# A hybrid encoder layer on one core: a staged opening, a third PSUM bank for projections, and a job order that passes blocked jobs

## The chip, the cores and the metric

The kernel runs on one core of one Trainium2 chip. The time is the device time of one execution in microseconds; here it is told as the median of several runs. The core has five engines, each with its own instruction queue, worked in order: TensorE (matmul, PE in the rows), VectorE (DVE), ScalarE (ACT), GpSimd (POOL) and SyncE (SP), which issues the DMA transfers. Matmuls write to PSUM, which has eight banks; VectorE and ScalarE read them from there.

## The reference

One step of a one-layer streaming encoder for 1024 prompt rows and 64 rows of a running stream, model width 1024, all in float32:

```
mod = silu(c) @ w_ada + b_ada           -> sh1, sc1, gt1, sh2, sc2, gt2
h   = rmsnorm(x) * (1 + sc1) + sh1
P   = h @ w_in                           # q, k, v | x, B, C | z gates | decays | merge gates
q, k, v, xs, B, C = silu(causal_dwconv4(...))
o   = gated_delta(l2norm(q), l2norm(k), v, g, beta)     # 8 heads, chunked, triangular solve
o   = rms(o) * gdn_norm * silu(z_g)
y   = ssd(xs, dt, A, B, C) + D * xs                     # 32 heads in 8 groups, chunked
y   = rms(y * silu(z_s)) * ssd_norm
x   = x + gt1 * (sigmoid(ga) * (o @ P_a) + sigmoid(gb) * (y @ P_b)) @ w_out
h2  = rmsnorm(x) * (1 + sc2) + sh2
u_a, u_v = causal_dwconv3(h2 @ w_up)
x   = x + gt2 * (silu(u_a) * u_v) @ w_down
return rmsnorm_final(x), and the new states of convolutions, delta net and SSD
```

## The kernel before

Both streams stand side by side as 1088 columns, channels on partitions. A projection makes 128 output channels: for each of three column segments (364, 364, 360) eight k tiles, and for each of these three matmuls, since weights and activations are split into two fp32r parts (high and low) and the product of the two low parts is left out. So a projection is 72 matmuls, a segment 24, and each segment fills one PSUM bank, which its `evac` reads.

**Opening.** x (eight tiles of 128 channels) is loaded first, then the weights of the modulation, in groups of four 512 KB loads. Each x tile is squared on ScalarE, and TensorE sums all eight squares over partitions with a matrix of ones, in fp32. From the sums come r0 = rsqrt (Ln and Exp). `ada` makes a modulation group: 32 matmuls per load pair, a copy, a transpose, an add. `norm_mod` makes the two parts of h for one x tile. The first two projections (`early_w`: the decays' small weights and the first K) run k tile by k tile while h comes, two k tiles (a pair) after each modulation group.

**Phase 1.** A list of jobs, one projection each: K, Q, V of the eight delta-net heads, B, C, X, x of the eight SSD groups, and 40 gate projections (24 z gates, 16 merge gates), which depend on nothing. The convolution of a mixer job runs in its `evac` on ScalarE and VectorE. Between the matmuls of the jobs stand the mixers' own matmuls: for each head an inverse (`gdn_inverse`: three kk batches, a 32-wide triangular solve on VectorE, four block steps), a scan over nine chunks (`gdn_scan`), the norm of o (`o_norm`, with a sum over partitions in `rsqrt_row`), for each group `ssd_mix`. Only TensorE's order is written out by hand: `weave` runs these generators against a planned clock, in which a step is due when the time in the table `LAT` has passed since its last one. `pick` chooses the next job: the first of the list when its condition holds, else a gate, up to `AHEAD` (3) gates more than the list's own F places; then the blocked job all the same. The other engines' orders come from a list scheduler.

PSUM before: two banks pj for projections, one each gk, gs (delta net), sa, sy (SSD), n and nv (kk batches, block steps and modulation, in turn).

**After phase 1** the gated outputs are multiplied by the two branch matrices and `w_out` (`project`, with `bank()` giving the banks in turn), then follow the norm, `up`, the convolution and `down`. The sums of the norms there used n and nv.

Of the kernel before, what the change touches and what calls it, by code (L numbers as in the profile page):

```python
# [20 lines left out]
P = 128  # L21
# [3 lines left out]
NC = 9  # L25
# [8 lines left out]
LAT = {"pre": 9.5, "dec": 1.6, "dec2": 27.6, "g0": 0.8, "e": 11.0, "kk": 1.0, "solve": 68.0, "inv": 1.8,  # L34
       "r": 1.6, "u": 1.7, "s": 2.5, "on": 18.4, "v": 9.0, "e2": 27.6, "s0": 5.6, "d0": 5.0, "w": 6.0, "r1": 2.0, "r2": 2.0}
MAN = {mybir.EngineType.PE}
ORDER = ["KFBFQCFXFxFV", "FKBFQCXFxFV"]
LAST = "BCFXx" + "F" * 9
AHEAD = 3
# [8 lines left out]
def body(tc, I, O):  # L48
# [34 lines left out]
    act.activation(scil, ct, AF.Tanh, scale=0.5)  # L83
# [9 lines left out]
    def ada(sc, g, ws, row, tag):  # L93
# [3 lines left out]
        for k0 in range(0, KT, 2):  # L97
            w = ws()
            sp.dma_start(w, I["wada"][g, :, k0:k0 + 2, :])
# [167 lines left out]
    def project_steps(w, x, evac):  # L267
# [5 lines left out]
        for si, (s, e) in enumerate(SEGS):  # L273
            ps = tl(pp, [P, 364], "pj", bufs=2)
# [43 lines left out]
    with ExitStack() as c1:  # L318
# [6 lines left out]
        hx = [tl(hp, [P, 2, T], f"h{k}", F32R) for k in range(KT)]  # L325
# [9 lines left out]
        for k in range(KT):  # L335
            sp.dma_start(xs[k], I["xT"][k])
# [3 lines left out]
        wb = [tl(gp, [P, TW], "k", bufs=2) for _ in range(2)] + [tl(gp, [P, 1024], "Ub"), tl(gp, [P, TW], "q", bufs=2)]  # L340
        wb += [sgt("bm"), tl(gp, [P, TC], "NU", bufs=2)]
        wb = [w[:, 0:1024].rearrange("p (k c) -> p k c", c=512) for w in wb]
        nwb = [0]

        def next_wb():
            nwb[0] += 1
            return wb[(nwb[0] - 1) % len(wb)]
        sc = padded_silu(tl(sg, [P, 256], "xw", bufs=2))
        r0 = tl(gp, [P, TC], "NU", bufs=2)
        a1 = tl(cst, [P, KT, 2], "a1")  # L350
        early_w = []
        with tc.manual_schedule(engines=MAN):
            nps = [tl(pp, [P, 364], t) for t in ("gs", "sa", "sy")]
            for k in range(KT):
# [6 lines left out]
            early = [[tl(pp, [P, 364], t, bufs=2 if t == "pj" else 1) for t in tags]  # L361
                     for tags in (("pj", "pj", "gk"), ("gs", "sa", "sy"))]
            for p in range(5):
                if p < 4:
                    ada(sc, p, next_wb, tl(gp, [P, P], "r"), "nv")
                    norm_scale(a1, wnm, 0, p)
                if p == 0:
                    early_w += [load_w(I["wsmall"]), load_w(I["win"][K0])]
                    continue
                ks = (2 * p - 2, 2 * p - 1)  # L370
                for k in ks:
                    for s, e in SEGS:
                        norm_mod(hx[k], xs[k], xs[k], r0, a1, k, 0, s, e, 0)
                for i in range(2):
                    for k in ks:
                        for si, (s, e) in enumerate(SEGS):
                            whi, wlo = early_w[i]
# [136 lines left out]
        def rsqrt_row(buf, eps):  # L514
# [3 lines left out]
            ps = tl(pp, [P, 364], "n")  # L518
# [20 lines left out]
        def kq_steps(w, h, j):  # L539
            yield from need(lambda: h < 2 or (heads[h - 2].norm.done if j else heads[h - 2].scanned))  # L540
# [763 lines left out]
```

## Time and profile before

| what | value |
|---|---|
| three runs, median (lowest to highest) | 2832.57 us (2831.6 to 2836.66) |
| profiled execution, its own time / span | 2831.39 / 2829.6 us |
| TensorE matmul busy | 2752.4 us, 97% of the span |
| VectorE / ScalarE / GpSimd busy | 1862.4 / 1247.5 / 201.9 us |
| moved by DMA | 266.75 MB |

Busy time is an average over stages with different limits. Phase 1 ends at about 1590 us; what follows is not touched but for the banks in which sums and modulation groups stand. In a stage where TensorE is busy nearly throughout, its gaps and the granted clock (1.00 is 2.4 GHz, half of it 1.2) are what is left to look at. A "releaser" is what ended a wait, inferred from the semaphores.

### The profile page before, as it was taken

How to read it: one execution, taken by the hardware profiler on the slowest of the kernel's cores; microseconds unless marked ns; L12 is line 12 of the kernel's file. 1: busy time of each engine (PE TensorE's matmuls, PEld its weight loads, DVE VectorE, ACT ScalarE, POOL GpSimd, SP SyncE). 2: the span in 40 equal slices, each digit the busy share in tenths (PEclk: the TensorE clock that was granted, in tenths of full speed). 3: DMA queues.
4: the chain of work that ended last, by engine and by line, in shares of the span. 5: the costliest groups of instructions: out<-in, count | busy, mean ns of one | idle time of the engine just before them, and what ended most of it. 6: DMA issues, size and time to landing. Idle time of an engine off the chain costs nothing.

```text
span 2829.6 us, 49056 instructions
## 1 busy us (share of the span) xinstructions
PE 2752.4 (97%) x18718; PEld 2654.6 (94%) x18718; DVE 1862.4 (66%) x4008; ACT 1247.5 (44%) x2847; POOL 201.9 (7%) x565
## 2 busy tenths in 40 slices
PE   7999999999999999999999999999999999999998
PEld 6999898999989999999999899999899999999998
DVE  4787687786877868678645657543675555555556
ACT  5634554554545444454443434312444242424244
POOL 0100111011101101111000000000010000000000
PEclk9999999999999999999999999999999999999999
DMA  6322313223232233222234766443211111111112
GB/s 221 96 74 76 117 53 117 70 82 104 81 97 81 82 94 99 78 85 79 79 99 146 245 204 204 139 147 93 90 47 49 45 46 38 53 38 53 38 60 72
DMA packets 204365, 266.75 MB, mean 94 GB/s; under 512 B 42522, under 2 KB 136410, under 8 KB 204130
## 3 DMA queue, kind: packets, MB, share of 16 engines
q1 hardware_dynamic: 204130, 263.62, 29.5%
q8 instruction: 147, 2.41, 0.4%
q14 instruction: 88, 0.72, 0.1%
HBM read 217.38 MB, written 46.13 MB: 93 GB/s over the span
## 4 chain that ended last, share of the span: by engine, by line
PE 80%; DVE 12%; DMA 4%; ACT 3%; issue 2%; POOL 0%; SPq 0%; DVEq 0%; ACTq 0%; POOLq 0%
PE pj L223 28%; PE pj L144 13%; PE gk L144 6%; PE gs L144 6%; PE sy L144 6%; PE sa L144 6%; PE sy L223 3%; DVE prod L615 3%; DVE Xb L618 2%; DMA wada<-in_wada 1%; PE gk L223 1%; DVE x L494 1%; PE n L223 1%; PE gs L223 1%; PE sa L227 1%
## 5 line engine op out<-in xcount | busy, mean ns | idle before, releaser
L223 PE MATMUL pj<-h,whi 128*128 128x364 f32 x4560 | 1157.5, 335 | 19.3 <-DVE fz L869 14.3
L223 PEld LDWEIGHTS pj<-h,whi 128*128 128x128 f32 x4560 | 792.9, 189 | 34.5 <-DVE fz L869 17.4
L223 PE MATMUL pj<-h,wlo 128*128 128x364 f32 x2280 | 749.2, 329 | 0.0
L223 PEld LDWEIGHTS pj<-h,wlo 128*128 128x128 f32 x2280 | 430.1, 189 | 0.0
L111 ACT CAST whi<-wraw 128x512 fp32r<-128x512 f32 (+1 forms) x386 | 234.5, 617 | 378.3 <-PE gs L144 145.5
L144 PE MATMUL pj<-op,whi 128*128 128x364 f32 (+1 forms) x1504 | 374.5, 329 | 0.0
L112 DVE TENSOR_TENSOR wlo<-wraw,whi 128x512 fp32r<-128x512 f32 (+1 forms) x386 | 263.0, 690 | 107.9 <-ACT whi L111 100.7
L144 PEld LDWEIGHTS pj<-op,whi 128*128 128x128 f32 x1504 | 266.5, 188 | 1.4 <-issue 0.2
L144 PE MATMUL pj<-op,wlo 128*128 128x364 f32 (+1 forms) x752 | 247.6, 329 | 0.0
L1096 DVE SCALAR_TENSOR_TENSOR acc<-buf,wfc,acc 128x364 f32<-128x364 f32 (+1 forms) x264 | 156.5, 596 | 97.9 <-ACT acc L1094 93.8
L144 PE MATMUL gk<-op,whi 128*128 128x364 f32 x752 | 191.2, 333 | 0.9 <-ACT op L185 0.6
L144 PE MATMUL gs<-op,whi 128*128 128x360 f32 x752 | 189.9, 331 | 0.0
L144 PE MATMUL sy<-op,whi 128*128 128x364 f32 x752 | 188.9, 331 | 0.0
L144 PE MATMUL sa<-op,whi 128*128 128x364 f32 x752 | 188.3, 330 | 0.0
L796 ACT ACTIVATE E<-E,ngam 128x128 f32<-128x128 f32 x288 | 96.4, 394 | 103.3 <-POOL E L793 101.9
L144 PEld LDWEIGHTS pj<-op,wlo 128*128 128x128 f32 x752 | 141.2, 188 | 0.5 <-issue 0.2
L144 PEld LDWEIGHTS gk<-op,whi 128*128 128x128 f32 x752 | 133.8, 189 | 4.6 <-DVE op L186 1.3
L144 PEld LDWEIGHTS gs<-op,whi 128*128 128x128 f32 x752 | 133.3, 188 | 2.6 <-ACT op L111 0.6
L144 PEld LDWEIGHTS sa<-op,whi 128*128 128x128 f32 x752 | 132.9, 188 | 2.2 <-issue 2.2
L144 PEld LDWEIGHTS sy<-op,whi 128*128 128x128 f32 x752 | 132.9, 188 | 2.1 <-issue 1.2
L615 DVE TENSOR_TENSOR prod<-Xb,Ub 108x2 f32<-108x2 f32 (+30 forms) x248 | 124.3, 501 | 5.6 <-POOL Ub L608 1.7
L144 PE MATMUL sa<-op,wlo 128*128 128x364 f32 x376 | 124.0, 330 | 0.0
(413 smaller groups left out, 4521.1 us busy)
## 6 DMA issues: line engine op xcount, KB each, us to landing
wraw<-in_win SPq DMA_DIRECT2D x160, 256.0 KB
wraw<-in_wup SPq DMA_DIRECT2D x88, 256.0 KB
gi<-gdr SPq DMA_DIRECT2D x72, 256.0 KB
wada<-in_wada SPq DMA_DIRECT2D x32, 512.0 KB
op<-spz SPq DMA_DIRECT2D x24, 544.0 KB
wraw<-in_wdown SPq DMA_DIRECT2D x40, 256.0 KB
spz<-fz SPq DMA_DIRECT2D x48, 182.0 KB
gt<-spg SPq DMA_DIRECT2D x48, 182.0 KB
```

The source lines that it names most:

```text
L111: act.copy(hi, src)
L112: dve.tensor_tensor(out=lo, in0=src, in1=hi, op=ALU.subtract)
L144: pe.matmul(pss[si][:, :e - s], lhsT=a[:, k, :], rhs=xk[:, b, s:e], start=(k == 0 and n == 0), stop=(k == nk - 1 and n == 2))
L223: pe.matmul(out, lhsT=lhsT, rhs=rhs, start=start, stop=stop)
L227: pe.transpose(out, in_, idn)
L494: dve.scalar_tensor_tensor(out=u, in0=buf[:, s + i:e + i], scalar=wcv[:, ti, i:i + 1], in1=u, op0=ALU.mult, op1=ALU.add)
L615: dve.tensor_tensor(out=prv, in0=X[:, 0:i + 1, 0:n].rearrange("p j c -> p c j"), in1=U[:, 0:i + 1, i:i + 1].rearrange("p j o -> p o j").to ...
L618: dve.tensor_reduce(out=X[:, i, 0:n], in_=prv, axis=mybir.AxisListType.X, op=ALU.add)
L796: act.activation(E[:, a, :], E[:, a, :], AF.Exp, bias=ngam[:, c, 8 + 4 * g + a:9 + 4 * g + a], scale=-1.0)
L1096: dve.scalar_tensor_tensor(out=acc[:, c0:c1], in0=buf[:, i + c0:i + c1], scalar=wfc[:, ti, i:i + 1], in1=acc[:, c0:c1], op0=ALU.mult, op1= ...
```

## The change

Opening: the first modulation group's weights are loaded ahead of x, into the places that later hold h; behind x come the two early weights whole, and then the other three groups' weights. The squares of x tiles 0 to 5 and of 6 and 7 are added on VectorE, and TensorE sums the two results: 6 matmuls for 24. The table of Ln and Exp is loaded once, right after the first Tanh. `norm_mod` works on all columns at once (1024 and 64) rather than by segment. The group of pair p+1 comes ahead of the matmuls of pair p.

Banks: nv goes, pj has three banks. The kk batches, block steps and modulation groups all use n; the sum under o's norm uses a pj bank; the sums of the output projections come from the rotation of `bank()`. The last two block steps leave out the ninth chunk, whose block is zero.

Order: `pick` passes a blocked job of one mixer and takes the first job of the other mixer that may go (never past a job of its own kind), then a gate, with up to six ahead. Some times of `LAT` are longer. In the order that comes of it, eleven gate projections follow the last mixer projection, where five did.

```diff
-LAT = {..., "kk": 1.0, "solve": 68.0, "inv": 1.8,
+LAT = {..., "kk": 1.6, "solve": 74.0, "inv": 2.6,
-AHEAD = 3
+AHEAD = 6
...
-        tag = ("pj", "gk", "pj", "gs", "sa", "sy")[nbank[0] % 6]
-        return tl(pp, [P, n], tag, bufs=2 if tag == "pj" else 1)
+        tag = ("pj", "gk", "pj", "gs", "pj", "sa", "sy")[nbank[0] % 7]
+        return tl(pp, [P, n], tag, bufs=3 if tag == "pj" else 1)
...
-            ps = tl(pp, [P, 364], "pj", bufs=2)
+            ps = tl(pp, [P, 364], "pj", bufs=3)
...
+        aw = [ada_w(0)]
+        for k in range(KT):
+            sp.dma_start(xs[k], I["xT"][k])
+        early_w = []
+        for src in (I["wsmall"], I["win"][K0]):
+            raw = tl(gp, [P, TW], "k", bufs=2)[:, 0:1024].rearrange("p (k c) -> p k c", c=P)
+            sp.dma_start(raw, src)
...
+        aw += [ada_w(p) for p in range(1, 4)]
+        inst = act.preload_act_table_set("natural_log_exp_and_others")
...
+            ada_h(0)
             for k in range(KT):
-                q = tl(cv, [P, 1096], "buf", bufs=2)
-                act.activation(q[:, 0:T], xs[k], AF.Square)
-                for si, (s, e) in enumerate(SEGS):
-                    pe.matmul(nps[si][:, :e - s], lhsT=ones, rhs=q[:, s:e], start=(k == 0), stop=(k == KT - 1))
+                k0 = 0 if k < 6 else 6
+                q = sq[k][:, 0:T] if k in sq else sqb[k % 4][:, 0:T]
+                act.activation(q, xs[k], AF.Square)
+                if k != k0:
+                    dve.tensor_tensor(out=sq[k0][:, 0:T], in0=sq[k0][:, 0:T], in1=q, op=ALU.add)
+                if k in (5, 7):
+                    for si, (s, e) in enumerate(SEGS):
+                        pe.matmul(nps[si][:, :e - s], lhsT=ones, rhs=sq[k0][:, s:e], start=(k == 5), stop=(k == 7))
...
+            for p in range(4):
+                for k in (2 * p, 2 * p + 1):
+                    hx.append(tl(hp, [P, 2, T], f"h{k}", F32R))
+                    norm_mod(hx[k], xs[k], xs[k], r0, a1, k, 0, 0, T, 0)
+                if p < 3:
+                    ada_h(p + 1)
...
-            ps = tl(pp, [P, 364], "n")
+            ps = tl(pp, [P, 364], "pj", bufs=3)
             for i in range(3):
                 mm(ps[32 * i:32 * i + 32, :], ones[:, 0:32], buf[:, 364 * i:364 * i + 364], True, True)
...
-                ps = tl(pp, [P, 4, P], ("n", "nv")[c0 // 4 % 2])
+                ps = tl(pp, [P, 4, P], "n")
...
+            if not jobs:
+                return fill.pop(0) if fill else None
+            seen = set()
+            for n, j in enumerate(jobs):
+                if j is not None and j[1] not in seen:
+                    gdn = j[1] in (kq_steps, v_steps)
+                    if j[3]():
+                        return jobs.pop(n)
+                    seen.update((kq_steps, v_steps) if gdn else (ssd_steps,))
+            if fill and ahead[0] < AHEAD:
+                ahead[0] += 1
+                return fill.pop(0)
+            return jobs.pop(0)
...
-            return tl(pp, [P, 512], ("n", "nv")[ptag[0] % 2])
+        ps_any = bank
```

How the instructions stand, at three places. First SyncE at the start of the program, before (v, q, gi, E, bm, cm and x are the eight x tiles; k, Ub, q, bm, NU take modulation weights):

```order
L336 DMA v_106<-in_xT 128x1088
L336 DMA q_107<-in_xT 128x1088
...
L336 DMA x_26_113<-in_xT 128x1088
L65 DMA ident_122<-in_ident 128x128
L65 DMA bada_124<-in_bada 128x48
L65 DMA wnm_126<-in_wnm 128x8
L99 DMA k_128<-in_wada 128x1024
```

and after (h_22 and h_23 are places of h, which hold the first group's weights; k_126 and k_130 take the early weights):

```order
L65 DMA ident_106<-in_ident 128x128
L65 DMA bada_108<-in_bada 128x48
L65 DMA wnm_110<-in_wnm 128x8
L345 DMA h_22_112<-in_wada 128x1024 x2
L345 DMA h_23_113<-in_wada 128x1024 x2
L352 DMA v_98<-in_xT 128x1088
...
L352 DMA x_18_105<-in_xT 128x1088
L356 DMA k_126<-in_wsmall 128x1024
L356 DMA k_130<-in_win 128x1024
L345 DMA h_30_134<-in_wada 128x1024 x2
```

The three small loads and four loads of modulation weights have moved ahead of x; the early weights stand right behind it.

Second TensorE at the block steps of head 1's inverse, before (n and nv are its banks, prod and Ub its operands; sa and sy are SSD chunks, pj projections):

```order
L223 MATMUL pj_3320<-h_18_105,wlo_2960 128x360
L223 MATMUL n_3400<-prod_2585,NU_2238 32x32 x18
L223 MATMUL sa_3421<-cm_1750,bm_1251 128x128
...
L223 MATMUL nv_3462<-NU_2238,Ub_2594 32x32 x2
...
L223 MATMUL n_3493<-prod_2585,NU_2238 64x64 x8
L223 MATMUL nv_3503<-prod_2585,NU_2238 64x64
L223 MATMUL sa_3510<-cm_1750,bm_1251 128x128
...
L223 MATMUL n_3539<-NU_2238,Ub_2594 64x64 x8
```

and after:

```order
L226 MATMUL n_3556<-prod_2707,NU_2313 32x32 x18
L226 MATMUL pj_3534<-h_73_522,whi_3426 128x364 x2
...
L226 MATMUL n_3600<-NU_2313,Ub_2716 32x32 x2
...
L226 MATMUL pj_3584<-h_68_433,whi_3426 128x364 x2
...
L226 MATMUL n_3658<-prod_2707,NU_2313 64x64 x8
L226 MATMUL pj_3648<-h_63_344,whi_3426 128x360 x2
...
L226 MATMUL n_3706<-NU_2313,Ub_2716 64x64 x8
```

Between the steps of the same inverse stood SSD chunks alone; now 18 matmuls of projections stand in each of the three gaps.

Third TensorE at the kk batches of head 0, before (rows of k over k into n, nv, n):

```order
L223 MATMUL n_1260<-k_683 128x128 x4
L223 MATMUL pj_1256<-h_12_99,whi_1144 128x364 x2
...
L223 MATMUL pj_1256<-h_14_101,wlo_1145 128x364
L223 MATMUL nv_1275<-k_683 128x128 x4
L223 MATMUL pj_1256<-h_15_102,whi_1144 128x364 x2
...
L223 MATMUL pj_1256<-h_17_104,wlo_1145 128x364
L223 MATMUL n_1290<-k_683 128x128
```

and after:

```order
L226 MATMUL n_1197<-k_620 128x128 x4
L226 MATMUL pj_1193<-h_58_255,whi_1081 128x364 x2
...
L226 MATMUL pj_1193<-h_67_426,wlo_1082 128x364
L226 MATMUL n_1215<-k_620 128x128 x4
L226 MATMUL pj_1193<-h_68_433,whi_1081 128x364 x2
...
L226 MATMUL pj_1237<-h_57_248,wlo_1082 128x364
L226 MATMUL n_1241<-k_620 128x128
```

The batches have one bank instead of two, and twelve projection matmuls between them instead of nine.

## Rows read from the trace of the kernel before

**Rows 1.** Windows by stretch: length, busy us (instructions) by engine, clock, DMA share, GB/s

```profile
0.00:70.00 70.00, 52.69 (x452) 43.13 (x453) 33.30 (x88) 40.08 (x68) 2.01 (x14) 0.93 0.62 221
70.00:290.00 220.00, 217.65 (x1497) 211.75 (x1497) 170.94 (x394) 107.51 (x261) 19.80 (x54) 1.00 0.27 82
290.00:340.00 50.00, 43.91 (x387) 39.17 (x383) 30.78 (x75) 25.46 (x69) 6.91 (x13) 0.86 0.46 133
340.00:1540.00 1200.00, 1173.79 (x8433) 1125.29 (x8432) 878.98 (x1986) 589.12 (x1470) 125.69 (x303) 1.00 0.28 87
1540.00:1620.00 80.00, 75.38 (x507) 70.51 (x506) 53.93 (x123) 34.04 (x81) 7.60 (x5) 0.98 0.76 257
1620.00:2040.00 420.00, 411.12 (x2778) 389.92 (x2777) 236.39 (x481) 139.94 (x287) 0.00 (x0) 1.00 0.47 151
```

**Rows 2.** Waits of TensorE, 60 to 1540 us: us in total, times, longest us

```profile
PE pj L223 <- DVE fz L869: 14.3, 10, 3.4
PE pj L223 <- ACT buf L484: 4.6, 2, 2.8
PE n L223 <- DVE prod L631: 2.7, 3, 1.7
```

**Rows 3.** Timeline, SyncE's DMA issues in the opening: start us, us, instruction

```profile
1.19 0.42 SPq L336 DMA_DIRECT2D v<-in_xT  x1
```

**Rows 4.** Windows, 10 to 20 us

```profile
10.00:20.00 10.00, 10.00 (x33) 6.18 (x32) 0.00 (x0) 5.71 (x6) 0.00 (x0) 1.00 1.03 401
```

**Rows 5.** Timeline, ScalarE in the opening

```profile
4.95 1.11 ACT L356 ACTIVATE buf<-v 128x1088 f32<-128x1088 f32 x1 [2.21 <-DMA v<-in_xT]
...
20.97 1.28 ACT L168 ACT_TABLE_LOAD   x1
```

**Rows 6.** Timeline, TensorE in the opening

```profile
6.11 1.58 PE L358 MATMUL gs<-buf,ones 128*128 128x364 f32 x2 [6.11 <-ACT buf L356]
...
12.28 0.78 PE L358 MATMUL gs<-buf,ones 128*128 128x364 f32 x2
...
30.00 1.08 PE L102 MATMUL nv<-k,xw 128*32 128x128 f32 x16
...
39.94 0.96 PE L379 MATMUL pj<-h,whi 128*128 128x364 f32 x2
...
70.06 0.49 PE L223 MATMUL pj<-h,whi 128*128 128x364 f32 x2
```

**Rows 7.** Timeline, VectorE: a 64-wide step and a 1024-wide one

```profile
43.70 0.28 DVE L183 SCALAR_TENSOR_TENSOR gi<-gi,a,NU 128x64 f32<-128x64 f32 x1
...
437.63 1.22 DVE L672 TENSOR_TENSOR gi<-gi,q 128x1024 f32<-128x1024 f32 x1
```

**Rows 8.** Timeline, TensorE near 310 us (idle before and its releaser in brackets)

```profile
309.61 0.75 PE L223 MATMUL n<-prod,NU 32*32 32x32 f32 x34 [1.74 <-DVE prod L631]
```

**Rows 9.** Timeline, ScalarE and TensorE near 435 us

```profile
431.71 2.74 ACT L561 ACTIVATE E<-E,ngam 128x128 f32<-128x128 f32 x9
...
437.10 0.46 ACT L867 ACTIVATE fz<-pj 128x364 f32<-128x364 f32 x1
...
439.35 0.60 PE L223 MATMUL pj<-h,whi 128*128 128x360 f32 x2 [3.39 <-DVE fz L869]
```

**Rows 10.** Windows, at two of the waits for a pj bank

```profile
435.00:439.00 4.00, 0.96 (x6) 0.66 (x4) 4.00 (x8) 3.33 (x10) 0.00 (x0) 1.00 0.12 34
...
1131.00:1143.00 12.00, 9.19 (x47) 8.89 (x46) 11.76 (x20) 8.56 (x24) 0.56 (x2) 0.86 0.20 58
```

**Rows 11.** Timeline, TensorE and VectorE at a kk batch of head 6

```profile
1068.12 1.06 PE L223 MATMUL n<-k 128*128 128x128 f32 x8
...
1071.41 0.68 DVE L584 TENSOR_TENSOR NU<-n,NU 128x512 f32<-128x512 f32 x1
```

**Rows 12.** Timeline, TensorE near 1580 us

```profile
1583.79 0.46 PE L223 MATMUL sa<-cm,bm 128*128 128x128 f32 x2 [3.89 <-DVE xw L817]
```

**Rows 13.** Chain that ended last: start us, us, what

```profile
1477.32 38.35 PE pj L223 x231
```

More of the change, by code (lines that the diff above doesn't have):

```diff
@@ L81, in body @@
     scil = tl(cst, [P, KT, 2], "scil")
-    act.activation(scil, ct, AF.Tanh, scale=0.5)
+    tanh_c = act.activation(scil, ct, AF.Tanh, scale=0.5)
     dve.scalar_tensor_tensor(out=scil, in0=scil, scalar=1.0, in1=ct, op0=ALU.add, op1=ALU.mult)
@@ L324, in body @@
         cv = c1.enter_context(tc.tile_pool(name="cv", bufs=1, side="right"))
-        hx = [tl(hp, [P, 2, T], f"h{k}", F32R) for k in range(KT)]
+        hx = []
         def sgt(tag):
@@ L334, in body, with ada_w @@
         xs += [sgt(t)[:, 0:T] for t in ("bm", "cm", "x0", "x1")]
-        for k in range(KT):
-            sp.dma_start(xs[k], I["xT"][k])
+        def ada_w(p):
+            ts = [tl(hp, [P, 2, T], f"h{2 * p + i}") for i in range(2)]
+            ws = [ts[i // 2][:, i % 2, 0:1024].rearrange("p (k c) -> p k c", c=512) for i in range(4)]
+            for i, w in enumerate(ws):
+                sp.dma_start(w, I["wada"][p, :, 2 * i:2 * i + 2, :])
+            return ws
         ident = load([P, P], I["ident"], "ident")
@@ L348, in body @@
+        early_w = []
+        for src in (I["wsmall"], I["win"][K0]):
+            raw = tl(gp, [P, TW], "k", bufs=2)[:, 0:1024].rearrange("p (k c) -> p k c", c=P)
+            sp.dma_start(raw, src)
+            hi, lo = (tl(wp, [P, KT, P], t, F32R) for t in ("whi", "wlo"))
+            early_w.append((raw, hi, lo))
+        aw += [ada_w(p) for p in range(1, 4)]
         sc = padded_silu(tl(sg, [P, 256], "xw", bufs=2))
+        inst = act.preload_act_table_set("natural_log_exp_and_others")
+        tc.add_manual_dep(inst.ins, tanh_c.ins.name,
+                          mybir.DependencyInfo(mybir.DependencyClass.NoSync, mybir.DependencyReason.DATA),
+                          reason="table set after the tanh")
@@ L349, in body, with ada_h @@
         r0 = tl(gp, [P, TC], "NU", bufs=2)
         a1 = tl(cst, [P, KT, 2], "a1")
-        early_w = []
+        def ada_h(p):
+            with first():
+                ada(sc, p, aw[p], tl(gp, [P, P], "r"), "n")
+                norm_scale(a1, wnm, 0, p)
         with tc.manual_schedule(engines=MAN):
+            ada_h(0)
             nps = [tl(pp, [P, 364], t) for t in ("gs", "sa", "sy")]
+            sq = {0: tl(cv, [P, 1096], "buf", bufs=2), 6: tl(cv, [P, 1096], "buf", bufs=2)}
+            sqb = [tl(cv, [P, 1096], "sq"), tl(gp, [P, TW], "q", bufs=2), sgt("bm"), tl(gp, [P, TC], "NU", bufs=2)]
@@ L359, in body @@
+                if k in (5, 7):
+                    for si, (s, e) in enumerate(SEGS):
+                        pe.matmul(nps[si][:, :e - s], lhsT=ones, rhs=sq[k0][:, s:e], start=(k == 5), stop=(k == 7))
             for si, (s, e) in enumerate(SEGS):
                 rms_act(r0[:, s:e], nps[si][:, :e - s])
[L361 to L375, printed above, removed]
+            for raw, hi, lo in early_w:
+                for k in (0, 4):
+                    split(hi[:, k:k + 4], lo[:, k:k + 4], raw[:, k:k + 4])
@@ new lines, in body @@
+            early = [[tl(pp, [P, 364], t, bufs=3 if t == "pj" else 1) for t in tags]
+                     for tags in (("pj", "pj", "pj"), ("gs", "sa", "sy"))]
+            for p in range(4):
[4 more added lines that the diff above has]
+                    ada_h(p + 1)
+                for i, (_, whi, wlo) in enumerate(early_w):
+                    for k in (2 * p, 2 * p + 1):
@@ L539, in kq_steps @@
         def kq_steps(w, h, j):
-            yield from need(lambda: h < 2 or (heads[h - 2].norm.done if j else heads[h - 2].scanned))
+            yield from need(lambda: h < 2 or ((heads[h - 2].norm and heads[h - 2].norm.done) if j else heads[h - 2].scanned))
             d = tl(gp, [P, TW], ("k", "q")[j], bufs=2)
@@ L550, in v_steps @@
         def v_steps(w, h):
-            yield from need(lambda: h == 0 or heads[h - 1].norm.done)
+            yield from need(lambda: h == 0 or (heads[h - 1].norm and heads[h - 1].norm.done))
             v = tl(gp, [P, TW], "v")
@@ L907, in pick @@
         def pick():
[L908 to L920 removed]
+            while jobs and jobs[0] is None:
+                jobs.pop(0)
+                if ahead[0] > 0:
+                    ahead[0] -= 1
+                elif fill:
+                    return fill.pop(0)
+            if not jobs:
[11 more added lines that the diff above has]
+            return jobs.pop(0)
         def main():
@@ L1008, in next_ada @@
             g = groups.pop(0)
[L1009 removed]
+            ada(sc, g, lambda: tl(op, [P, 2, 512], "wada"), tl(op, [P, P], "row", bufs=1), "n")
             if g in (4, 5):
```

57 lines of the change are left out of this document (17 added, 40 removed).

## The prediction

> **What bounds the kernel now.** I read the stages first: busy time and granted clock by stretch [rows 1]. From 70 us on TensorE is busy nearly throughout: idle are 2.4 us of 220, 6.1 of 50 (290 to 340 us), 26.2 of 1200 (340 to 1540) and 4.6 of 80 (1540 to 1620), against 17.3 of the first 70. VectorE is at 73% in the long stretch, ScalarE at 49%. So phase 1 is a queue of TensorE work whose amount the change hardly alters, and the time can only come from gaps and from stretches at the lower of the two clock levels. Second, who ends TensorE's gaps between 60 and 1540 us [rows 2]: 14.3 + 4.6 us are waits of a projection (tile pj) for the reader of its PSUM bank, 2.7 us waits for the solve. Third, the opening and the places of the longest gaps in order of time [rows 3 to 9, 12, 13].
>
> The sum is made against the profiled execution: span 2829.6 us and 1.8 around it, 2831.4 us; the median of the three runs, 2832.6, is 1.2 above. A measurement tells from no change what is over 0.2%, 5.7 us.
>
> **The change part by part.**
>
> *Opening.* Before, the two early projections start at 39.94 us and hand over at 70.06 [rows 6]: 30.1 us for 144 matmuls and two modulation groups between them. After, the same 144 matmuls have the same two groups between them, so I keep the 30.1 us and ask when the first can start. It needs r0 (the scale of RMSNorm) and group 0's and group 1's turn on TensorE.
> The stream: before, the first x tile (0.56 MB, 1.4 us at 401 GB/s [rows 4]) is issued at 1.19 us and its Square starts at 4.95 [rows 3, 5], so data flow from about 3.5. After, three small loads go ahead (0.45 us each) and then group 0's 2.1 MB: flow from 4.9, and 2.1 + 4.5 MB take 16.4 us, last x at 21.3. Its Square takes 1.1 us [rows 5]; its add is 1088 wide, like the 1024-wide row of 1.22 us [rows 7], so 1.3. Then three sums at 0.6 us each, or 1.2 at the lower clock, which is what a pair took at 12.3 and at 6.1 us [rows 6], and a last Ln and Exp of about 0.5 each, as a 364-wide ScalarE step takes [rows 9]. The four table loads of 1.28 us that stood among them [rows 5] go to one ahead. r0 is whole at 26.5 to 28.5 us. First halves of h: a 1024-wide VectorE step (1.25), the 64-wide one (0.2), ScalarE 1.0, VectorE 1.3: 30.5 to 32.5.
> The other condition: small weights and K0 (1.05 MB) and group 1 (2.1 MB) follow x: 29.2 us, then its last quarter (0.5 to 0.9 us at either clock [rows 6]), a copy and a transpose, about 1: 31. So the pair loop starts at about 31.5 instead of 39.9: **-8 us**. Bounds: -12 (r0 early, the loop's start at the higher clock) and 0 (the lower clock throughout, and h late for each pair). VectorE's work for a pair of x tiles is four 1024-wide and four 64-wide steps [rows 7], 6.1 us, beside a pair's 36 matmuls of 0.166 us (38.35 us for 231 [rows 13]), 6.0, and a group's turn of 1.5 to 2.5 us, so it hides; if each pair waited a microsecond, 4 us would go.
>
> *Third pj bank.* The waits of rows 2 are 18.9 us, the longest 3.4. What a wait is, shows at 435 us [rows 9]: nine Exps of the decay hold ScalarE for 2.7 us, the gate's Tanh comes at 437.1 only, VectorE's read of the bank after it, and TensorE goes on at 439.35. A third bank lets a reader be one segment later, 24 matmuls, 4.0 us: more than the longest wait. Three of these waits (966, 1133, 1311 us) are followed by a stretch at the lower clock: 0.86 over 12 us, as the second of them shows [rows 10], 1.7 us each, 5.1. Of the 24.0 us I take **-20**, since the sums under o's norm now take a turn in the same banks. That costs at each of 8 heads at most one wait as long as the longest of before, 27 us, and at least nothing: beside the short sum there is still a whole segment between two uses, so I take **+1**.
>
> *Job order.* From 290 to 340 us TensorE loses 6.1 us idle and 14% of the clock, 7.0 us, together 13.1 [rows 1]. There V of head 1 waits for the norm of head 0, gates run out at three ahead, and the block steps of head 1's inverse stand bare behind one another, the first waiting 1.7 us for the solve [rows 8]. After, projections stand between them (the second pair of order fences). I leave the 1.1 us that 50 us of the long stretch lose: **-12**, bounds -13 and -8. What is late next: nothing that the order shows; the gates used here are missing from no later place, since eleven stand behind the last mixer job where five did. That covers the tail as well: from 1540 to 1620 us 4.6 us idle and 2% of the clock are lost, 6.2 us, most of it in one wait of 3.9 us [rows 12] of the last SSD chunks. In its place comes the load of operands 6 and 7 of the output projection, whose buffers come free with the last projection only, with about 10 us of matmuls as cover: **-3**, bounds -6 and +5.
>
> *One bank for the inverse.* nv is gone: each kk batch, and each block step, waits for the reader of the one before. The block steps read what the step before wrote, so they waited already. For kk, the worst row has the batch end at 1069.2 us and VectorE's product at 1072.1, 2.9 us later [rows 11]. Two waits in each of 8 heads: 46 us if all were like it and nothing stood between; nothing if the 1.6 us planned between them covers. The order shows twelve projection matmuls between, 2.0 us (third pair), so **+2.5**. solve at 74 takes the 2.7 us of rows 2: **-2**. The last chunk's two block steps fall away: 16 short matmuls, 0. Later adas in one bank and the output projections' sums in the rotation: TensorE's waits of 1620 to 2040 us are 8.9 us in all [rows 1]; 0, bounds -3 and +5.
>
> Sum: -8 - 20 + 1 - 12 - 3 + 2.5 - 2 = -41.5, so 2789.9 for a profiled execution, and **2791 us** for the median.
>
> **The rivals.**
> *The third bank gives little* (0.17). While the wait at 435 lasts, VectorE is busy 4.0 of 4 us, and 11.8 of 12 at 1131 [rows 10]: if the readers themselves are behind, a later segment waits instead, or the split of the weights does. For it: those rows. Against: the waits are 10 and 2 in number, not a train of them, and none in rows 2 is for weights. A quarter of the 24 us comes: 2791 + 14 = 2805. The Trainium skill, "TensorE: Matmul & The Clock Gate", section "HAM oscillation — how this bites in real kernels", reports of one kernel that double-buffering PSUM "gave no further gain"; the rows here show waits for banks, which speaks against it holding.
> *The opening gives nothing* (0.12). x now stands behind 2.1 MB, and TensorE idles until the sums, so that they and the groups run at the lower clock; at the upper end of each step the loop starts near 39: 2799. For it: the lower clock at 6 us. Against: the chain of four terms still ends before 32. The Trainium skill, "DMA: Bandwidth & Descriptors", section "Where 436 GB/s comes from", lets loads from HBM run at about 358 GB/s; the row of 10 to 20 us has 401, and the row decides. By the page x would land 2 us later and the sum would be 2793.
> *The idle moves to the end* (0.05). Gates used early leave the last chain bare, and the 12 us come back: 2803. Against: the eleven gates behind the last job.
> *Slower: the single bank n* (0.06). Three kk batches and the block steps of a head pass through one bank in TensorE's own order, and behind a waiting matmul stand the projections. If the 48 waits (6 in each of 8 heads) average over 0.9 us, the gain of 44 us without this term is gone; at 1.5 us it is 72 - 44 = 28 us slower, 2860. For it: 2.9 us in rows 11, when VectorE is full. Against: the 2.0 us of matmuls between batches.
>
> **How the numbers follow.** The forecast holds with 0.60. Its own range is 2778 to 2803 (pj -24 to -12, opening -12 to -3, tail and kk 5 us either way). With the rivals the range is 2772 to 2817: below lie all gains at their bounds, above the slower case and two rivals together. Faster by over 0.2%: the forecast and the first three rivals less 0.04 for two or three of them together, 0.89; within 0.2%: 0.05, with a share of the slower case at its turning point; slower: 0.06.
>
> **What would show it.** Opening: the first projection behind the early ones starts at 61 to 63 us. pj: waits of pj for fz and buf under 5 us in all, clock 1.00 from 340 to 1540. Order: no idle over 1 us near 300. Bank n: waits of n for the kk product under 4 us. It is wrong if pj waits remain at the same places, if n waits pass 10 us, or if a new wait, for weights or for operands 6 and 7, exceeds 5 us.

## The result, and the profile after

The changed kernel takes 2800.4 us (median of 4 runs, 2797.7 to 2800.9) against 2832.1 before (4 runs on the same chip): a ratio of 0.9885, 95% interval 0.9869 to 0.9901, or 31.7 us less. The profiled execution went from 2831.4 to 2797.7 us, 33.7 less; the forecast's sum was 41.5 less.

Where the time went is seen between three points that both programs have: the first projection behind the early ones (70.06 us before [rows 6], 64.73 after), the first sum under the norm behind `w_out` (2011.7 and 1977.9), and the end. The opening gave 5.3 us, the middle 28.5, the rest nothing (817.9 and 818.0). The middle by the windows view, first of before, then of after (length, then busy us of PE, PEld, DVE, ACT, POOL, then granted clock, DMA share and rate):

```profile
70.06:2011.70 1941.64, 1896.96 (x13374) 1817.19 (x13374) 1344.73 (x2996) 878.67 (x2128) 159.99 (x375) 0.99 0.34 108
```

```profile
64.73:1977.90 1913.17, 1882.37 (x13342) 1808.10 (x13342) 1346.82 (x2996) 874.25 (x2113) 149.59 (x375) 1.00 0.34 109
...
64.73:290.00 225.27, 222.18 (x1544) 215.48 (x1544) 174.55 (x408) 116.34 (x279) 23.81 (x60) 1.00 0.26 83
290.00:340.00 50.00, 49.00 (x419) 46.19 (x418) 31.93 (x66) 24.24 (x64) 5.16 (x11) 1.00 0.46 144
340.00:1505.00 1165.00, 1144.24 (x8336) 1095.24 (x8336) 889.22 (x2026) 582.18 (x1466) 120.61 (x304) 1.00 0.28 88
1505.00:1555.50 50.50, 50.50 (x306) 50.50 (x305) 24.44 (x47) 17.79 (x38) 0.00 (x0) 1.00 0.70 242
1555.50:1590.00 34.50, 33.84 (x200) 32.72 (x199) 20.99 (x42) 13.72 (x27) 0.00 (x0) 1.00 0.81 278
```

TensorE's idle time (length less busy) fell from 44.7 to 30.8 us, 13.9; its busy time by 14.6, though only 32 matmul records (the 16 short matmuls of the ninth chunk) went: most of it is the clock. The stretch of 290 to 340 us lost 6.1 us and 14% of the clock [rows 1]; now 1.0 us and nothing. The end of phase 1 lost 4.6 us and 2%; now 0.7. The long stretch lost 26.2 us and still loses 20.8; its clock of 1.00 hides one fall, behind the wait for wlo named below:

```profile
980.00:990.00 10.00, 6.21 (x25) 5.79 (x24) 7.36 (x15) 2.28 (x5) 0.49 (x3) 0.70 0.46 136
```

Who ends its gaps, by the waits view of TensorE from 60 to 1560 us, to be held against [rows 2]:

```profile
PE pj L226 <- DVE fz L893: 5.8, 4, 2.4
PE sy L226 <- DVE yc L878: 4.3, 4, 1.4
PE gs L226 <- DVE r L736: 4.1, 7, 1.2
PE pj L226 <- DVE wlo L115: 3.8, 1, 3.8
PE n L226 <- ACT Ub L664: 1.9, 2, 1.4
PE n L226 <- DVE prod L656: 1.4, 2, 1.0
...
PE n L226 <- DVE NU L609: 0.9, 1, 0.9
```

Waits for a pj bank fell from 18.9 to 5.8 us, nearly as forecast; but a wait for wlo (at 981 us), more for yc and for Ub stand where none or less stood. What is left for pj looks like what [rows 9] showed; ScalarE, VectorE and TensorE about 485 us, by the timeline:

```profile
481.31 2.15 ACT L586 ACTIVATE NU<-NU,ngam 128x128 f32<-128x128 f32 x7
483.36 2.74 ACT L586 ACTIVATE E<-E,ngam 128x128 f32<-128x128 f32 x9
...
487.06 0.46 ACT L891 ACTIVATE fz<-pj 128x360 f32<-128x360 f32 x1
...
488.38 1.22 DVE L696 TENSOR_TENSOR gi<-gi,q 128x1024 f32<-128x1024 f32 x1
489.51 0.52 DVE L893 SCALAR_TENSOR_TENSOR fz<-fz,pj 128x360 f32<-128x360 f32 x1
...
490.09 0.60 PE L226 MATMUL pj<-h,whi 128*128 128x360 f32 x2 [2.40 <-DVE fz L893]
```

The Tanh of a segment done at 479.7 us starts at 487.1, behind 17 Exps of two decay masks and a wider one, and VectorE's read that frees the bank stands behind another product. The opening, by the timeline:

```profile
21.40 1.58 PE L386 MATMUL gs<-buf,ones 128*128 128x364 f32 x2 [8.82 <-DVE buf L383]
...
24.98 0.78 PE L386 MATMUL gs<-buf,ones 128*128 128x364 f32 x2
...
28.24 0.50 ACT L172 ACTIVATE NU<-NU 128x360 f32<-128x360 f32 x1
...
32.97 0.95 PE L404 MATMUL pj<-h,whi 128*128 128x364 f32 x2
...
38.49 0.50 PE L404 MATMUL gs<-h,whi 128*128 128x364 f32 x2
```

TensorE had been idle since 12.6 us. The first sums run at the lower clock by the times of their matmuls (1.58 us for a pair, 0.78 later; the trace has no clock record before 24.8 us) and keep the last three waiting, whose add is done at 23.95; r0 is whole at 28.7, the first pair of early projections starts at 32.97 and is at the lower clock until 38.4.

### The profile page after: what moved, and what is told of

Its sections match the earlier page's. It is cut to its first block, busy times and chain, and to the rows that moved or that the text cites. A ratio compares the mean times of both kernels' runs of the same rounds, so it can differ in the third digit from the quotient of the medians.

```text
span 2795.9 us, 48799 instructions
## 1 busy us (share of the span) xinstructions
PE 2728.5 (98%) x18650; PEld 2639.7 (94%) x18650; DVE 1868.0 (67%) x3982; ACT 1235.1 (44%) x2813; POOL 191.2 (7%) x565
## 4 chain that ended last, share of the span: by engine, by line
PE 81%; DVE 9%; DMA 5%; ACT 2%; issue 1%; POOL 1%; SPq 0%; DVEq 0%; POOLq 0%; ACTq 0%
PE pj L226 30%; PE pj L147 16%; PE sy L147 6%; PE sa L147 6%; PE gk L147 5%; PE gs L147 5%; PE sy L226 3%; DVE prod L640 2%; DMA gi<-gdr 2%; DVE Xb L643 2%; PE n L226 1%; DMA wada<-in_wada 1%; PE gk L226 1%; PE gs L226 1%; PE pj L1217 1%
## 5 line engine op out<-in xcount | busy, mean ns | idle before, releaser
L147 PE MATMUL pj<-op,whi 128*128 128x364 f32 (+1 forms) x1904 | 476.7, 330 | 0.8 <-ACT op L188 0.6
L147 PEld LDWEIGHTS pj<-op,whi 128*128 128x128 f32 x1904 | 337.3, 188 | 6.7 <-issue 1.4
L147 PE MATMUL pj<-op,wlo 128*128 128x364 f32 (+1 forms) x952 | 312.5, 329 | 0.0
L147 PEld LDWEIGHTS pj<-op,wlo 128*128 128x128 f32 x952 | 178.8, 188 | 0.0
L147 PE MATMUL sy<-op,whi 128*128 128x364 f32 (+1 forms) x672 | 167.8, 330 | 0.0
L147 PE MATMUL gs<-op,whi 128*128 128x364 f32 (+1 forms) x652 | 164.1, 331 | 0.9 <-ACT q L1001 0.7
L147 PE MATMUL sa<-op,whi 128*128 128x364 f32 (+1 forms) x644 | 161.4, 330 | 0.0
L147 PE MATMUL gk<-op,whi 128*128 128x364 f32 (+1 forms) x640 | 159.5, 330 | 0.7 <-ACT op L114 0.7
L147 PEld LDWEIGHTS gk<-op,whi 128*128 128x128 f32 x640 | 113.3, 188 | 1.9 <-ACT op L114 1.0
L147 PE MATMUL sy<-op,wlo 128*128 128x364 f32 (+1 forms) x336 | 110.3, 328 | 0.0
```

The lines of the kernel that those rows point to most:

```text
L147: pe.matmul(pss[si][:, :e - s], lhsT=a[:, k, :], rhs=xk[:, b, s:e], start=(k == 0 and n == 0), stop=(k == nk - 1 and n == 2))
```

## The experiments

All start from the changed kernel and are timed beside the kernel before, whose median was 2832.6 to 2833.9 (2832.1 beside the changed kernel). "Middle" is the stretch defined above, with TensorE's idle time in it, in the profiled execution alone: that one lies 2.7 us below the median for the changed kernel and 3.2 above it for e1. "First" is where the middle begins; among runs with the same opening that is 64.2 to 65.5.

One edit of the change stands in no text ahead of the prediction. `ORDER` lists the jobs of a round, F being a place for a gate, and lost an F in every other round:

```diff
-ORDER = ["KFBFQCFXFxFV", "FKBFQCXFxFV"]
+ORDER = ["KFBFQCXFxFV", "FKBFQCXFxFV"]
```

No run takes this back. "Old order" in e3 and e10 is the old `pick` with three ahead on the new list, which is an order of neither kernel.

| run | median us | ratio to before (95%) | first | middle / idle |
|---|---|---|---|---|
| changed kernel | 2800.4 | 0.9885 (0.9869 to 0.9901) | 64.7 | 1913.2 / 30.8 |
| e1 two pj banks | 2822.9 | 0.9963 (0.9952 to 0.9975) | 65.1 | 1940.6 / 45.4 |
| e2 the same, with nv | 2822.1 | 0.9963 (0.9948 to 0.9978) | 65.2 | 1937.7 / 46.7 |
| e3 old `pick` | 2858.2 | 1.0091 (1.0076 to 1.0106) | 64.8 | 1977.2 / 74.9 |
| e5 old latencies | 2868.9 | 1.0118 (1.0102 to 1.0135) | 64.8 | 1987.0 / 75.3 |
| e10 old `pick` and latencies | 2836.0 | 1.0008 (0.9999 to 1.0017) | 65.3 | 1950.7 / 56.1 |
| e12 inv 1.8 alone | 2853.7 | 1.0078 (1.0055 to 1.0101) | 64.2 | 1971.4 / 67.4 |
| e4 old opening | 2807.1 | 0.9914 (0.9897 to 0.9930) | 71.3 | 1915.9 / 32.2 |
| e6 sums all by TensorE | 2804.9 | 0.9897 (0.9882 to 0.9911) | 68.5 | 1918.8 / 32.7 |
| e11 sums in pairs, h by segment | 2798.7 | 0.9883 (0.9868 to 0.9898) | 62.7 | 1914.3 / 32.0 |
| e7 Tanh ahead | 2798.7 | 0.9874 (0.9859 to 0.9889) | 64.6 | 1916.7 / 27.9 |
| e8 split ahead | 2810.9 | 0.9923 (0.9908 to 0.9938) | 65.5 | 1925.1 / 35.2 |
| e13 half the split on GpSimd | 2819.3 | 0.9952 (0.9938 to 0.9965) | 65.1 | 1934.9 / 43.6 |

### The banks (e1, e2)

```diff
-        tag = ("pj", "gk", "pj", "gs", "pj", "sa", "sy")[nbank[0] % 7]
+        tag = ("pj", "gk", "pj", "gs", "sa", "sy")[nbank[0] % 6]
...
-            ps = tl(pp, [P, 364], "pj", bufs=3)
+            ps = tl(pp, [P, 364], "pj", bufs=2)
...
```

> The changed kernel with two pj banks again (the eighth bank unused; everything else as changed, so also one bank n and the sums under o's norm in pj). Theory A (the third bank gave what the forecast took, and the shortfall is elsewhere): projections wait about 19 us for their banks instead of 5.8, three to five stretches fall to the lower clock, total 2818 to 2822. Theory B (the waits that the bank took away came back as others: waits for wlo, for yc and for Ub, because VectorE and ScalarE are behind): pj's waits go up by 13 us, the others go down by 4 to 8, total 2806 to 2812. Sums in pj are worth up to 8 us more here than with three banks if they take a turn that a reader needs.

Waits of e1:

```profile
PE pj L226 <- DVE fz L893: 27.0, 11, 4.4
PE sy L226 <- DVE yc L878: 4.8, 4, 1.4
...
PE pj L226 <- ACT buf L512: 2.0, 1, 2.0
...
PE pj L226 <- ACT fz L901: 1.2, 1, 1.2
```

It is 22 us slower, 1 us above theory A's range. TensorE's order in phase 1 is the same instruction for instruction, and the last 387.9 us of the middle, behind phase 1, differ by 1 us of idle time, so this is the bank in phase 1: pj's waits go from 5.8 to 30.2 us. Theory B has a part in it: the other named waits in these views fall by 8.0 us to 10.9, with the one for wlo gone and those for yc still there, so a third of what the bank takes off pj comes back elsewhere. pj's 30.2 us are also more than its 18.9 in the kernel before: the new order, with the sums under o's norm in the same banks, asks more of them than the old one did.

e2 adds nv (kk batches and block steps in n and nv by turns, as before):

> The kernel of the run before this one (two pj banks), and the eighth bank as nv again for the kk batches and the inverse's block steps. It differs from that by the single bank n alone. If the single bank costs what the forecast took, this is 2.5 us faster than two pj banks without nv; if the single bank is free (waits of n for the kk product are 0.9 us in the changed kernel's trace), 0 to 1 us; if it costs over 5 us, the forecast's term was too small.

It is 0.7 us faster, within the spread: the single bank is free or nearly so.

### Order and latencies (e3, e10, e5, e12)

```diff
-AHEAD = 6
+AHEAD = 3
...
-            for n, j in enumerate(jobs):
...
+                elif jobs[0][3]() or not fill or ahead[0] >= AHEAD:
+                    return jobs.pop(0)
...
```

> The changed kernel with the old choice of the next job (three gates ahead, no passing). Theory: the stretch around 290 to 340 us loses again 5 us idle and 7 us of clock, and the last SSD chunks stand bare again at the end of phase 1 (4 to 6 us): 2800.4 + 16 to 18 = 2817, less what the new order itself costs elsewhere. Rival: with three banks the same places are covered anyway, and it is at most 5 us slower; second rival: the new order brought the waits for wlo (3.8 us) and for yc (4.3), and without it these go, so that it is 8 to 10 us slower only.

Both sides were far off: 58 us slower. Waits of e3:

```profile
PE pj L226 <- DVE wlo L115: 21.2, 6, 5.1
PE n L226 <- DVE prod L656: 14.1, 2, 13.4
```

The 13.4 us end at 323 us: between 285 and 333 us no projection stands in TensorE's order, only mixer steps that wait for one another. So the latencies came next, with the old `pick` (e10) and with the new one (e5):

```diff
-LAT = {..., "kk": 1.6, "solve": 74.0, "inv": 2.6,
+LAT = {..., "kk": 1.0, "solve": 68.0, "inv": 1.8,
```

> The changed kernel with the old job order (three ahead) and the old latencies: the kernel before with only the new opening, three pj banks and the single bank n. Theory A (the third bank gives the same in either order, and the loss of the old order with new latencies was the latencies'): 2832.5 - 6.7 (opening) - 13 to -20 (bank) = 2806 to 2813. Theory B (the third bank gives only with the new order, because in the old order the split of the weights is late instead: 21.2 us of waits for wlo in the run with the old order): pj waits for wlo stay above 10 us, total 2822 to 2835. If it is as slow as with the new latencies (2858), the order alone is worth more than 50 us with three banks.

The time is 1 us past theory B's range: as slow as the kernel before, with a middle that is 9 us longer. pj's waits for fz are gone, and others stand there; below them the windows view of 290 to 340 us:

```profile
PE pj L226 <- DVE wlo L115: 18.7, 6, 4.8
PE n L226 <- DVE prod L656: 8.4, 4, 4.6
PE sa L226 <- ACT E L820: 6.4, 1, 6.4
```

```profile
290.00:340.00 50.00, 34.81 (x310) 30.09 (x309) 26.13 (x61) 22.54 (x58) 7.68 (x14) 0.76 0.35 108
```

In that stretch it loses 15.2 us idle and 24% of the clock, where the kernel before lost 6.1 and 14%. But e10 does not have the jobs of the kernel before in their order: with the old list its plan has them, job for job (counted, not run). So what the third bank gives in the old order is not shown, and theory B is not decided.

> The changed kernel with the old latencies (kk 1.0, solve 68, inv 1.8). Theory A (the forecast's small terms): the waits of n for the solve come back by 2 to 3 us, and with the kk batches closer together in the one bank n each waits up to 2.9 us: 2800.4 + 3 to 8 = 2804 to 2808. Theory B (the longer solve plans the inverse later, which delays the scan and starves later jobs, as the 13.4 us wait in the old order with the new latencies hints): the old latencies are as fast or up to 4 us faster, 2796 to 2801.

Neither theory holds: it is 68 us slower than the changed kernel. A count in the order of TensorE's instructions shows what the latencies did. The unit is a projection of 72 matmuls, of which phase 1 has 95 behind the early ones; the block steps of the inverses of heads 3 to 7 start after so many:

```
changed kernel   38.8 48.8 58.8 68.8 78.8   last scan ends 87.2, last SSD chunk 88.9
e5 old latencies 38.4 49.4 60.4 71.4 82.4                  91.5                 94.0
e12 inv 1.8      38.8 49.8 60.8 71.8 82.8                  91.5                 94.0
before           35.9 46.7 57.6 68.2 79.2                  87.9                 95.0
e10              34.7 45.7 56.7 67.7 78.7                  87.4                 91.3
```

A head takes ten projections in the changed kernel (seven mixer jobs and three gates) and eleven with the old latencies, where nearly nothing is left beside the last mixer steps. Eleven alone is not what is slow: e10 has it too, and the kernel before nearly so, from a start some three projections earlier, so that their last scans end at 87 to 88. Of the eight combinations of old and new values, only the two with both solve 74 and inv 2.6 give ten; with the old list the plan of the changed kernel has eleven too (counted, not run). To test what a single latency costs, e12 takes back one number:

```diff
-LAT = {..., "inv": 2.6,
+LAT = {..., "inv": 1.8,
```

> The changed kernel with one number undone: the planned latency of an inverse's block step, 1.8 instead of 2.6 (solve stays 74, kk 1.6). In the order so planned the inverses of heads 4 to 7 stand 11 projections apart instead of 10, the last scan ends with 3.5 projections left instead of 7.8, and the last SSD chunks with 1.0 instead of 6.1, as in the run with all three old latencies. Theory (these latencies decide between two orders, and the order decides the time): 2855 to 2870, like that run's 2869. Rival (a latency is worth about the waits that it plans for, 0.8 us for 3 steps of 8 heads): 2795 to 2812.

It is 53 us slower, 1 below the theory's range and far above the rival's. Windows of e12, then one of the changed kernel, then two waits of e12:

```profile
340.00:1500.00 1160.00, 1129.23 (x8106) 1084.22 (x8105) 855.55 (x1944) 573.54 (x1411) 116.23 (x297) 0.99 0.28 85
1500.00:1600.00 100.00, 87.83 (x603) 81.20 (x601) 43.04 (x105) 34.10 (x87) 4.83 (x7) 0.93 0.46 152
1600.00:1700.00 100.00, 87.92 (x565) 80.38 (x566) 65.72 (x137) 41.57 (x88) 0.00 (x0) 0.93 0.63 221
```

```profile
1500.00:1700.00 200.00, 196.44 (x1250) 188.90 (x1249) 111.32 (x221) 76.26 (x156) 0.00 (x0) 1.00 0.70 239
```

```profile
PE gk L147 <- ACT op L114: 16.6, 2, 12.1
PE sa L226 <- ACT fz L891: 12.2, 3, 4.1
```

24 us are idle between 1500 and 1700 and 7% of the clock is lost, where the changed kernel has 3.6 us idle and the full clock; half of the 24 is one wait of the output projection for its first operands, which are made from the mixers' outputs. From 340 to 1500 us 31 us are idle against 21 in the changed kernel's 340 to 1505. That the late last scan causes the larger part is read from these places; no run moves it alone.

### The opening (e4, e6, e11)

e4 puts the old opening back (x first, groups in a ring, all sums on TensorE).

> The changed kernel with the old opening (x first, groups of wada in a ring behind the sums, small and K0 loaded late, table loads where they fall), with three pj banks and bank n. Theory: only the start moves, the first projection behind the early ones is at 70 us instead of 64.7, and the total is 5.3 us above 2800.4: 2805.7 (2804 to 2808). Rival: what is gained in the opening is lost or doubled later, because the weights and VectorE's work stand differently against each other from 65 us on: 0 or 10 us.

The middle begins 6.5 us later and is 2.7 longer; the medians differ by 6.7. The opening's gain carries through.

```diff
-                if k != k0:
-                    dve.tensor_tensor(out=sq[k0][:, 0:T], in0=sq[k0][:, 0:T], in1=q, op=ALU.add)
-                if k in (5, 7):
-                    ...
+                for si, (s, e) in enumerate(SEGS):
+                    pe.matmul(nps[si][:, :e - s], lhsT=ones, rhs=q[:, s:e], start=(k == 0), stop=(k == KT - 1))
```

> The changed kernel with the opening's sums of squares taken by TensorE for each x tile as it lands (24 matmuls in place of VectorE's six adds and 6 matmuls, as the kernel before had them). Theory (TensorE's idle time from 12.1 to 21.4 us in the changed opening puts the sums, group 1 and the first pair of early projections at the lower clock): behind the last Square at 22.6 us come three sums at the full clock (0.9 us instead of 4.3), r0 is whole at 25.5 instead of 28.7, the first pair starts at about 30 and keeps the full clock: the first later projection starts at 59 to 61 us instead of 64.7, total 2800.4 - 4 to -5.5 = 2795 to 2796.5. Rival: group 1's weights (last quarter at 29.2 us) bind then, and the clock falls anyway: -1 to -2.

It is 4.5 us slower, because the expectation took half the price of a sum. One is two matmul records, 0.61 us from start to start at the full clock:

```profile
29.00 0.77 PE L382 MATMUL sa<-buf,ones 128*128 128x364 f32 x2
29.61 0.77 PE L382 MATMUL sy<-buf,ones 128*128 128x360 f32 x2
```

24 of them end at 30.3 instead of 26.9 us. With that price e11 makes two edits: it sums in four sets of three, and makes the first pair of h by segment:

```diff
+                if k % 2:
...
+                    dve.tensor_tensor(out=q0, in0=q0, in1=q, op=ALU.add)
...
+                        pe.matmul(nps[si][:, :e - s], lhsT=ones, rhs=q0[:, s:e], start=(k == 1), stop=(k == KT - 1))
...
-                    norm_mod(hx[k], xs[k], xs[k], r0, a1, k, 0, 0, T, 0)
+                    for s, e in SEGS if p == 0 else [(0, T)]:
+                        norm_mod(hx[k], xs[k], xs[k], r0, a1, k, 0, s, e, 0)
```

> The changed kernel with two edits in the opening: the squares of x tiles are added two by two and summed by TensorE in four sets of three (it was six in one set and two in another), and the first pair of h is modulated segment by segment as r0 comes. Theory: behind the last add at 24 us come three sums at the full clock (0.61 us each, as the run with all sums on TensorE showed), r0's first segment is there at about 27, the early projections start at 31 instead of 33 and at the higher clock, the first later projection starts at 61 to 62.5 instead of 64.7: 2800.4 - 2 to -4 = 2796.5 to 2798.5. Rival (the clock falls whatever is done, because TensorE has to wait for h in either case, and VectorE's 1.6 us of additional work for the pair delays the second): 64 to 66 us, no gain.

The middle begins at 62.7, 2.0 us earlier and 0.2 behind the theory's range:

```profile
24.22 0.88 PE L385 MATMUL gs<-buf,ones 128*128 128x364 f32 x2 [0.68 <-DVE buf L383]
...
31.91 0.58 PE L404 MATMUL pj<-h,whi 128*128 128x364 f32 x2
...
33.22 0.81 PE L404 MATMUL pj<-h,whi 128*128 128x360 f32 x2
...
36.51 0.49 PE L404 MATMUL gs<-h,whi 128*128 128x364 f32 x2
```

The first pair starts at the higher clock (a pair of matmuls takes 0.58 us), is at the lower from about 33 us (0.81), and back at 36.4. The median is 1.7 us lower, which these intervals don't tell from nothing.

### What is left of the waits (e7, e8, e13)

```diff
-                act.activation(th[:, :e - s], ps[:, :e - s], AF.Tanh, scale=0.5)
                 with first():
+                    act.activation(th[:, :e - s], ps[:, :e - s], AF.Tanh, scale=0.5)
```

> The changed kernel with the gate's Tanh at the high priority that its VectorE product already has. Theory (the four remaining waits of pj for fz, 5.8 us, are the Tanh standing behind some 17 Exps of two decay masks on ScalarE: at 481 to 487 us it starts 7.6 us after its segment is done): pj waits for fz under 2 us, total 2800.4 - 3 to -5 = 2795 to 2797. Rival (VectorE's solve steps and the 1.2 us product of gi are what the read is behind, as they stand directly ahead of it at 488 us): the waits stay above 4 us, total within 2 us of 2800.4.

The waits for fz are gone, and the time is the same within the spread. Others grew:

```profile
PE pj L226 <- DVE wlo L115: 5.3, 3, 3.9
PE n L226 <- ACT Ub L664: 4.3, 2, 2.5
```

e8 puts the weights' split under `first()` instead:

> The changed kernel with both halves of the weight split (ScalarE's cast to whi, VectorE's wlo) at the high priority. Theory (the 3.8 us wait for wlo at 981 us is the split standing behind the solve's last steps and the convolution's sums on VectorE, and nothing else): no wait of pj for wlo is left, others stay, total 2800.4 - 3 to -5 = 2795.5 to 2797.5. Rival (VectorE is the bound in these stretches, so what goes ahead makes something else late): the sum of TensorE's named waits stays within 3 us of 24.9, total within 2 us of 2800.4, as with the Tanh put ahead (2798.7, where the waits for fz went from 5.8 to 0 and those for wlo and Ub rose by 3.9).

The waits for wlo are gone, and the kernel is 10 us slower: the solve comes late.

```profile
PE n L227 <- DVE prod L657: 7.5, 5, 2.4
PE sy L227 <- DVE yc L879: 6.2, 4, 3.0
PE pj L227 <- DVE fz L894: 4.4, 3, 1.8
```

In e7 and e8 the waits on VectorE and ScalarE change places. e13 takes work off VectorE (in `load_w`, the second half of each split of phase 1):

```diff
+                pool.tensor_tensor(out=lo[:, k0:k0 + n], in0=raw[:, :n], in1=hi[:, k0:k0 + n], op=ALU.subtract)
```

> The changed kernel with half of phase 1's wlo subtractions (one of the two of each projection's weights, some 93 of 0.69 us, 64 us of VectorE's time) on GpSimd, which is busy for 7% of the span and does a 128x512 select in 0.79 us. TensorE's order is the same. Theory (what is left of the waits in the long stretch, 20.8 us, and what moved about when Tanh or split were put ahead, is VectorE with more work queued than the planned latencies allow): with 5% of the stretch taken off VectorE the named waits of TensorE from 60 to 1560 us fall from 24.9 to 12 to 18 us, total 2800.4 - 6 to -12 = 2788 to 2794, the fastest version. Rival A (the waits are set by each chain's own length, not by what else VectorE has to do): within 2 us of 2800.4. Rival B (GpSimd's subtraction is slow, or slows VectorE while it runs, so that wlo comes late instead): waits of pj for wlo over 10 us, total above 2806.

It is 19 us slower: rival B by its time, and by its mechanism in part, since VectorE is slowed, but waits of pj for wlo stay at 3.8 us. GpSimd's subtraction takes 1.44 us, and VectorE is busy for 887.9 us of 340 to 1505 us against 889.2, though it has 84 instructions less there; over the whole middle 1350.7 against 1346.8 with 94 less. Lines view of e13, GpSimd and VectorE (busy us, mean ns), and its window:

```profile
L126 POOL TENSOR_TENSOR wlo<-wraw,whi 128x512 fp32r<-128x512 f32 x95 | 137.0, 1442 | 221.9 <-ACT whi L125 179.9 <-issue 22.2 <-PE n L230 13.5
...
L523 DVE SCALAR_TENSOR_TENSOR k<-buf,wcv,k 128x364 f32<-128x364 f32 (+1 forms) x72 | 50.0, 698 | 6.4 <-ACT k L521 4.4
```

```profile
340.00:1505.00 1165.00, 1139.29 (x8287) 1087.25 (x8286) 887.86 (x1942) 581.94 (x1465) 211.97 (x375) 1.00 0.29 86
```

and the same VectorE line in the changed kernel, with VectorE's own subtraction:

```profile
L519 DVE SCALAR_TENSOR_TENSOR k<-buf,wcv,k 128x364 f32<-128x364 f32 (+1 forms) x72 | 42.5, 594 | 3.5 <-ACT k L517 2.0
L115 DVE TENSOR_TENSOR wlo<-wraw,whi 128x512 fp32r<-128x512 f32 x374 | 254.9, 691 | 101.4 <-ACT whi L114 100.7
```

Theory and rival A are not decided by it, since VectorE was not relieved. No run is faster than the changed kernel by more than the measurement tells.

## Why the prediction was right, and where it was not

The measured 2800.4 lies 9 us above the forecast and 3 us below the upper end of its own range, 2803. That end is too low by its own terms: 8, 5 and 5 us above 2791 are 2809. The opening and the long stretch gave less than forecast, the stretch of 290 to 340 us what was forecast, the tail more; that the result is still inside the range is partly luck.

*Opening, -8 forecast, -5.3.* The order of events was right. The step that was mis-sized is r0, 28.7 us against an upper bound of 28.5: the first three sums ran at 1.2 GHz and kept the others waiting for 1.0 us, and ScalarE had two Exps to do ahead of the last Ln, so that 1.8 us stand between the last sum and r0 instead of 1.0. So the pair loop starts at 32.97, not 31.5. Group 1's turn, the other condition, came at 32.84 too and not at 31, its copy being behind ScalarE's steps for h. And "I keep the 30.1 us" failed: 31.8, because the first pair took 8.6 us where before it had taken 7.0 (39.94 to 46.91), at the lower clock for longer. e11, with TensorE at work from 16 us on, won back 2.0.

*Third bank, -20 + 1.* The waits went nearly as forecast (13.1 us of 18.9, and the clock with them), and e1 puts the bank at 22 us in the new order. But other waits came in the long stretch (3.8 us for wlo and 4.3 for yc, where neither stood): idle there fell by 5.4, where the idle part of the terms made 14 (20/24 of 18.9, less 1 and 2.5, plus 2 for the solve). That is the first rival's mechanism ("the split of the weights does") at part strength; e10's 18.7 us of waits for wlo show how far it can go in another order. The forecast gave that rival 0.17 as if it were a matter of yes or no. The case that the Trainium skill tells in "TensorE: Matmul & The Clock Gate", section "HAM oscillation — how this bites in real kernels", where a further PSUM buffer "gave no further gain", is not this one: e1's 22 us hang on one bank alone.

*Job order -12, tail -3, solve -2.* The stretch of 290 to 340 us gave 12.1, the end of phase 1 5.5; operands 6 and 7 did not come late. As an account of causes this part failed: the terms were summed as if each edit had its own. "solve at 74 takes the 2.7 us of rows 2: -2" was the worst. With inv as before, or all three latencies, the planner puts a head on eleven projections, and the kernel is 53 or 68 us slower than the changed one; solve alone was not run. The edit of `ORDER` had no term at all, though the ten projections a head and the eleven gates at the end hang on it too (counted, not run). And the parts do not add up: without the third bank the middle gains 1 us by the two profiles (1940.6 against 1941.6) and some 5 by the medians (e1, 10.3 less the opening), with it 28.5; undoing `pick` and the latencies and keeping the bank (e10) makes it 9 longer than before. The sum came near because its terms were read from the order of the whole change, the list's edit included.

*Single bank n, +2.5.* There are 0.9 us of waits for the kk product, and e2 is within 1 us. The slower rival, which rested on this bank, had no ground; the danger lay in the latencies and the order, which no rival named.

*The tests.* The first projection was to start at 61 to 63 us: it starts at 64.7, a miss. pj's waits were to be under 5 us: they are 5.8, at places like those of before, which was a sign of being wrong. No idle over 1 us near 300, n's waits for the kk product under 4 and no new wait over 5 held. The clock of 1.00 from 340 to 1540 held as a mean, with 0.70 from 980 to 990.

## What to carry to other kernels

Where a planner sets the order from a list of jobs and a table of latencies, a latency can be worth far more than the wait that it plans for: it is a switch between orders. A bank is worth what it is in one order. So read the order of the whole change, test its parts by leaving one out, and count in the order of the instructions whether a run has put back what it is meant to put back. Where several steps queue on one helper engine (VectorE is busy for 76% of the long stretch), a wait taken off one can come back at another, so forecast the stretch's idle time, not the waits by name.

## What the runs showed of the hardware that was not expected

GpSimd takes 1442 ns for the subtraction that VectorE does in 691, and while it works some of VectorE's own instructions lengthen. The convolution steps on K, whose means above mix the segments, take 594 and 698 ns; of e13's 168 convolution steps on a last segment (363 columns), the 55 that a subtraction overlaps by over 0.1 us take 1168 ns on average and the 113 others 593. The gate's product, which reads one operand from PSUM, takes 524 ns in its nine overlaps and 526 elsewhere. The Trainium skill, "GPSIMD Engine Reference", section "Engine selection", puts two-input operations there at about twice VectorE's time, which the rows bear out (2.09); "SBUF — State Buffer", section "Terms", says that the two engines share a port pair which one of them holds for a whole instruction, and the longer steps agree with that.

An fp32 sum of 364 columns costs TensorE 0.61 us at 2.4 GHz and 1.2 to 1.4 at 1.2 GHz. And a wait can cost more than itself: in e7 idle time is 2.9 us less than in the changed kernel and busy time 6.4 us more, with the granted clock at 0.83 from 1160 to 1180 us, where a wait of 2.5 us stands at 1161 to 1163; the changed kernel has 0.5 us of wait there and a clock of 1.00.
